# The last stage of a two-layer decoder trunk: its first loads and splits moved ahead, its outputs issued by GpSimd, its norm products cut in pairs

## The chip, the cores and the metric

The kernel runs on one core of a Trainium2 chip. The metric is the time of one execution on the device in microseconds (us), lower is better. The engines are TensorE (PE, with its weight loads shown apart as PEld), VectorE (DVE), ScalarE (ACT), GpSimd (POOL) and SyncE (SP). SP only issues transfers here; ACT and POOL can issue them too, and such an issue stands in that engine's queue like any other instruction. Every queue is worked off in order.

## The reference

Two layers, each `x + mixer(RMSNorm(x))`, over 2048 tokens of width 1024; a last RMSNorm ends the trunk. Layer 0 is an mLSTM, layer 1 an RG-LRU. What the change touches is the second half of layer 1 and the last norm:

```python
xr, g = split(rmsnorm(x, ln_g[1]) @ w_in)            # two halves of width 1536
xc = causal_dwconv(xr)
r  = sigmoid(blockdiag(xc, w_a) + b_a); ig = sigmoid(blockdiag(xc, w_x) + b_x)
log_a = -8 * r * softplus(-lam); a = exp(log_a)
hs = linear_scan(a, sqrt(1 - exp(2*log_a)) * (ig * xc))
x  = x + (hs * silu(g)) @ w_out
out = x * rsqrt(mean(x*x) + eps) * final_g
```

## The kernel before

All matrix products are done in float32 as three products of rounded parts: an operand is split into `hi` (a cast on ACT, L720) and `lo` (a subtraction on DVE, L723), and `mm3` (L347 to L349) adds `hi*hi + hi*lo + lo*hi`. One weight tile of 128x128 against 512 tokens is thus three matmuls.

The stages follow one another: `phase_a1`, `phase_a2` (layer 0), `phase_b1` (output projection of layer 0 and input projection of layer 1), `phase_b2` (gates, scan, output projection and last norm). The change is in the end of `phase_b1` and in `phase_b2`.

**The end of phase_b1.** The input projection runs in groups of seven products (`Slab.group`). The last group makes the last four tiles of the branch `g`: `out(mi, ni, put)` of `g_out` lets `put` write the tile (a copy on ACT for tile (0,0), additions on DVE at L259 for the other three), then applies SiLU on ACT (L1155), and writes the tile to DRAM; for this last group POOL issues that write (L1157).

**phase_b2** goes over four blocks of 512 tokens. In a block there are eight gate steps `("g", b, i)`: step i needs one weight tile of the block-diagonal gates, 128x896 (`wg`, 21 matmuls); even steps make the r gate and the decay (L1286 to L1295), odd ones the input gate, the scan and the split result `yh`, `yl` (L1290 to L1304, then L720 and L723). There are 24 output columns `("r", b, i)`: column i needs one tile of `w_out`, 128x512 (`wr`, 12 matmuls), and the 24 columns make the two halves of the block's output. Columns lag the gates by five steps, and three columns follow each gate step.

*Weights.* `fetch` loads a raw tile on SP (L1232) and splits it. In block 0 POOL writes the split tile to DRAM (L1235), and the later blocks load it from there on SP (L1229). There is one raw buffer for `wg` and three for `wr`, two split buffers for `wg` and four for `wr`. `weights()` keeps three tiles fetched ahead, all with raised priority. `load(b, p)` brings three tiles of `xc` (768 KB): one transfer on SP (L1265), but for the first in the kernel, which is three transfers on POOL (L1262).

*The norm.* After a half's last column, `x2_out` loads four tiles of x on SP (L1345; eight buffers for two halves), adds the products and squares them. Three steps later come the sums and `rsqrt` on POOL (L343), three steps later the row of factors (`stats_rows`, copied on ACT at L1370), the eight products on DVE (L1372) and the eight writes of the result (L1373): on ACT, in the last block in turn on ACT and SP. This tail runs while the next block's columns call `next(run["r", b - 1])`, one piece at each column.

*The order.* The program is traced, and a planner puts each engine's instructions in an order by its own estimate of times and by priority (the program's order, raised by `high_priority`). Buffers are placed in SBUF pool after pool in the order in which the pools are opened, and the pools of phase_b2 lie over those of phase_b1; `reuse_waits="tile"` makes an access wait for the old tile under it alone. So the pool that is opened first lies over the first operands of phase_b1 (`u11`, `t2`, ...), which the last group reads first. `order(first, then)` (already used where phase_a2 begins) adds an edge that puts the instructions of `then` behind those of `first` on the same engine.

Of the kernel before, what the change touches and what calls it, by code (L numbers as in the profile page):

```python
# [7 lines left out]
F32 = mybir.dt.float32  # L8
F32R = mybir.dt.float32r
I32 = mybir.dt.int32  # L10
AF = mybir.ActivationFunctionType
# [3 lines left out]
P = 128  # L15
# [23 lines left out]
class Slab:  # L39
# [20 lines left out]
    def wk(self, name):  # L60
        return self.rg.tile([P, 516], F32, tag="wk", name=name, bufs=10)
# [233 lines left out]
class Trunk:  # L295
# [731 lines left out]
    def phase_b1(self, xT, wout, rwin, D):  # L1027

        tc, nc = self.tc, self.nc
        NG = 6  # L1030
        with ExitStack() as ctx:
            S = Slab(self, ctx, "g1")
            tp, rg, wk, psum = S.tp, S.rg, S.wk, S.psum
# [3 lines left out]
            order = [("w", k, 0) for _ in range(NTB) for k in range(16)]  # L1037
# [5 lines left out]
            ready = []  # L1043
# [104 lines left out]
            def g_out(m2, s):  # L1148
                def out(mi, ni, put):
                    m, n = m2 * 2 + mi, s * 2 + ni  # L1150
                    g = wk("g")[:, 0:TB]
                    put(g)

                    def rest():
                        nc.scalar.activation(g, g, AF.Silu)  # L1155
                        q = nc.gpsimd if s == 1 and m2 == NG - 1 else nc.scalar
                        q.dma_start(D["g"][m, :, n * TB:(n + 1) * TB], g)  # L1157
                    return rest
                return out
# [43 lines left out]
    def phase_b2(self, rgate, rwout, D, outT):  # L1203


        tc, nc = self.tc, self.nc
        NT = 12
        with ExitStack() as ctx:
            wp = ctx.enter_context(tc.tile_pool(name="w4", bufs=4, reuse_waits="tile"))
            tp = ctx.enter_context(tc.tile_pool(name="t4", bufs=2, reuse_waits="tile"))  # L1210
            pm = ctx.enter_context(tc.tile_pool(name="psB", bufs=8, space=PSUM, reuse_waits="tile"))
            steps = []
            lag = 5
# [5 lines left out]
            order = list(steps)  # L1219
            ready = []  # L1220

            def fetch(kind, b, i):

                m = 896 if kind == "g" else 512
                both = wp.tile([P, 2 * m], F32R, tag="w" + kind, name="w" + kind, bufs=2 if kind == "g" else 4)
                wh, wl = both[:, 0:m], both[:, m:2 * m]
                keep = D["gw" if kind == "g" else "ow"][i]
                if b > 0:
                    nc.sync.dma_start(both.bitcast(F32), keep)  # L1229
                    return wh, wl  # L1230
                raw = wp.tile([P, m], F32, tag="wr" + kind, name="wr", bufs=1 if kind == "g" else 3)
                nc.sync.dma_start(raw, rgate[i // 2, :, i % 2 * 896:(i % 2 + 1) * 896] if kind == "g" else  # L1232
                                  rwout[i % NT, :, i // NT * 512:(i // NT + 1) * 512])
                self.split_into(wh, wl, raw, "a", "v")
                nc.gpsimd.dma_start(keep, both.bitcast(F32))  # L1235
                return wh, wl

            def weights():

                with tc.high_priority():  # L1240
                    while order and len(ready) < 3:
                        ready.append(fetch(*order.pop(0)))
                return ready.pop(0)

            def psum(name):
                return pm.tile([P, TB], F32, tag="mm", name=name)
# [7 lines left out]
            def load(b, p):  # L1254

                c = tp.tile([P, 3, TB], F32, tag="xc", name="xc", bufs=4)
                hi = tp.tile([P, 3, TB], F32R, tag="xch", name="xch")
                lo = tp.tile([P, 3, TB], F32R, tag="xcl", name="xcl")
                src = D["xr"][p * 3:p * 3 + 3, :, b * TB:(b + 1) * TB]
                if b == 0 and p == 0:  # L1260
                    for t in range(3):
                        nc.gpsimd.dma_start(c[:, t], src[t])  # L1262
                        self.split_into(hi[:, t], lo[:, t], c[:, t], "a", "v")
                else:
                    nc.sync.dma_start(c, src.rearrange("k p t -> p k t"))  # L1265
                    self.split_into(hi, lo, c, "a", "v")
                return c, hi, lo

# [42 lines left out]
            def block(b):  # L1311

                ys = blocks[b] = []
                if b == 0:
                    with tc.high_priority():
                        xs = load(b, 0)
                else:
                    xs = load(b, 0)
                for p in range(4):
                    nxt = load(b, p + 1) if p < 3 else None  # L1320
                    yield from gates(b, p, xs, ys)
                    xs = nxt

            def x2_out(b):

                bs = slice(b * TB, (b + 1) * TB)
                ys = blocks[b]
                x2, sacc = [], None
                for half in range(2):
                    acc = [psum("acc") for _ in range(4)]  # L1330
                    last = b == NTB - 1 and half == 1
                    held = []
                    for k in range(NT):
                        held.append((k, weights()))
                        if not last or k < NT - 3 or k == NT - 1:
                            for m in range(4):
                                ms = slice(m * P, (m + 1) * P)
                                for i, (wh, wl) in held:
                                    self.mm3(acc[m], wh[:, ms], wl[:, ms], ys[i][0], ys[i][1], i == 0, i == NT - 1)
                            held = []  # L1340
                        if k < NT - 1:
                            yield
                    for m in range(4):
                        x = tp.tile([P, TB], F32, tag="x2", name="x2", bufs=8)
                        nc.sync.dma_start(x, D["x1"][half * 4 + m, :, bs])  # L1345
                        nc.vector.tensor_tensor(x, x, acc[m], op=ALU.add)
                        x2.append(x)
                        if sacc is None:
                            sacc = tp.tile([P, TB], F32, tag="sacc", name="sacc", bufs=1)
                            nc.scalar.activation(sacc, x, AF.Square)  # L1350
                        else:
                            sq = tp.tile([P, TB], F32, tag="sq", name="sq")
                            nc.scalar.activation(sq, x, AF.Square)
                            if last and m == 3:
                                sums = [sacc, sq]
                            else:
                                nc.vector.tensor_tensor(sacc, sacc, sq, op=ALU.add)
                                sums = [sacc]
                    yield
                rc = tp.tile([P, 4], F32, tag="rc", name="rc")  # L1360
                yield
                yield
                self.stats_sum(tp, pm, sums, rc, "mm")
                yield
                yield
                yield
                rb = self.stats_rows(pm, rc, "mm")
                if not last:
                    pb, rb = rb, tp.tile([P, TB], F32, tag="rb", name="rb", bufs=1)
                    nc.scalar.copy(rb, pb)  # L1370
                for m in range(KD):
                    nc.vector.scalar_tensor_tensor(x2[m], x2[m], self.v("gf", m), rb, op0=ALU.mult, op1=ALU.mult)  # L1372
                    (nc.scalar if m % 2 or not last else nc.sync).dma_start(outT[m, :, bs], x2[m])  # L1373

            run = {}
            for kind, b, i in steps:
                if kind == "g":
                    if i == 0:
                        run["g", b] = block(b)
                    next(run["g", b])  # L1380
                else:
                    if i == 0:
                        run["r", b] = x2_out(b)
                    next(run["r", b])
                    if b > 0:
                        next(run["r", b - 1], None)
# [94 lines left out]
```

## Time and profile before

| | |
|---|---|
| median of 3 runs | 3046.7 us (3042.29 to 3050.06) |
| the profiled execution, its own time | 3045.92 us |
| its span in the trace | 3044.1 us |
| PE busy | 2921.0 us (96%) |
| DVE busy | 2083.8 us (68%) |
| ACT busy | 1470.6 us (48%) |
| POOL busy | 195.4 us (6%) |

Times below are us from the start of the span. The page cuts the span in 40 slices; the last stage begins in slice 34, where PE falls to 7 tenths. The views of the trace that follow are the timeline (start, duration, engine, line, what it writes and reads, and in brackets how long the engine stood idle before it and what it waited for), the busy time of each engine in given stretches with the granted clock of PE, groups of instructions by line, and transfers by line.

### The profile page before, as it was taken

How to read it: one execution, taken by the hardware profiler on the slowest of the kernel's cores; microseconds unless marked ns; L12 is line 12 of the kernel's file. 1: busy time of each engine (PE TensorE's matmuls, PEld its weight loads, DVE VectorE, ACT ScalarE, POOL GpSimd, SP SyncE). 2: the span in 40 equal slices, each digit the busy share in tenths (PEclk: the TensorE clock that was granted, in tenths of full speed). 3: DMA queues.
4: the chain of work that ended last, by engine and by line, in shares of the span. 5: the costliest groups of instructions: out<-in, count | busy, mean ns of one | idle time of the engine just before them, and what ended most of it. 6: DMA issues, size and time to landing. Idle time of an engine off the chain costs nothing. (4 is left out here: it accounts for less than half of the span.)

```text
span 3044.1 us, 43340 instructions
## 1 busy us (share of the span) xinstructions
PE 2921.0 (96%) x15730; PEld 2503.5 (82%) x15730; DVE 2083.8 (68%) x3555; ACT 1470.6 (48%) x2458; POOL 195.4 (6%) x409
## 2 busy tenths in 40 slices
PE   7999999999999999999999899999999997899997
PEld 5799987899988898989899777877888886688886
DVE  7766788534566687888888555687778374876663
ACT  6344545323344566666666323243445233865651
POOL 0111110000000011111110000001110000000000
PEclk9999999999999999999999999999999998999998
DMA  6766677667677544454443665566666656888865
GB/s 227 269 214 245 223 245 242 207 203 208 214 236 222 187 139 156 139 163 146 136 146 108 195 190 179 181 209 226 215 215 223 208 185 246 302 282 302 301 206 166
DMA packets 308662, 632.06 MB, mean 208 GB/s; under 512 B 27680, under 2 KB 106272, under 8 KB 308448
## 3 DMA queue, kind: packets, MB, share of 16 engines
q1 hardware_dynamic: 219328, 408.66, 43.2%
q10 hardware_dynamic: 58752, 106.98, 10.0%
q0 software_dynamic: 30368, 113.65, 9.5%
q8 instruction: 124, 2.03, 0.3%
q14 instruction: 90, 0.74, 0.1%
HBM read 407.74 MB, written 221.45 MB: 207 GB/s over the span
## 5 line engine op out<-in xcount | busy, mean ns | idle before, releaser
L720 ACT CAST s<-raw 128x512 fp32r<-128x512 f32 (+1 forms) x360 | 222.7, 621 | 497.5 <-PE acc L349 192.5
L723 DVE TENSOR_TENSOR s<-raw,s 128x512 fp32r<-128x512 f32 (+1 forms) x360 | 247.1, 689 | 94.7 <-ACT s L720 92.3
L347 PE MATMUL acc<-yh,s 128*128 128x512 f32 x512 | 203.0, 399 | 9.9 <-DVE x L1115 3.3
L348 PE MATMUL acc<-yl,s 128*128 128x512 f32 x512 | 203.5, 397 | 0.0
L349 PE MATMUL acc<-yh,s 128*128 128x512 f32 x512 | 203.1, 397 | 0.0
L347 PE MATMUL acc<-yh,wr 128*128 128x512 f32 x384 | 149.3, 397 | 15.1 <-DMA wr<-d_ow 7.7
L348 PE MATMUL acc<-yl,wr 128*128 128x512 f32 x384 | 151.2, 394 | 0.0
L349 PE MATMUL acc<-yh,wr 128*128 128x512 f32 x384 | 150.8, 393 | 0.0
L647 DVE SCALAR_TENSOR_TENSOR xc<-xm,vec,xc 128x512 f32<-128x512 f32 x192 | 140.3, 747 | 14.5 <-ACT xc L645 12.5
L720 ACT CAST s<-sum 128x512 fp32r<-128x512 f32 (+1 forms) x120 | 74.3, 620 | 153.0 <-PE pa L349 48.0
L347 PEld LDWEIGHTS acc<-yh,s 128*128 128x128 f32 x512 | 96.9, 190 | 35.0 <-DVE x L1115 4.4
L348 PEld LDWEIGHTS acc<-yl,s 128*128 128x128 f32 x512 | 97.2, 190 | 23.2 <-DVE yl L723 1.0
L349 PEld LDWEIGHTS acc<-yh,s 128*128 128x128 f32 x512 | 97.0, 189 | 22.7
L915 DVE SCALAR_TENSOR_TENSOR C<-C,dl,kv 128x516 f32<-128x516 f32 x112 | 83.7, 747 | 44.7 <-PE kv L349 44.6
L347 PE MATMUL gate<-xch,wg 128*128 128x512 f32 x224 | 92.7, 417 | 21.5 <-ACT wg L720 11.7
L647 DVE SCALAR_TENSOR_TENSOR xc<-xr,vec,xc 128x512 f32<-128x512 f32 x144 | 105.1, 747 | 7.3 <-ACT xc L645 6.3
L723 DVE TENSOR_TENSOR s<-sum,s 128x512 fp32r<-128x512 f32 (+1 forms) x120 | 82.6, 689 | 39.7 <-ACT s L720 38.2
L720 ACT CAST Ch<-C 128x516 fp32r<-128x516 f32 x120 | 74.8, 623 | 64.7 <-DVE da L933 48.1
L347 PE MATMUL pj<-vwh,xmh 128*128 128x512 f32 x256 | 103.1, 403 | 0.0
L347 PEld LDWEIGHTS acc<-yh,wr 128*128 128x128 f32 x384 | 72.7, 190 | 34.1 <-issue 8.1
L349 PE MATMUL pj<-vwh,xml 128*128 128x512 f32 x256 | 100.3, 392 | 0.0
L348 PE MATMUL pj<-vwl,xmh 128*128 128x512 f32 x256 | 100.0, 391 | 0.0
(429 smaller groups left out, 9435.9 us busy)
## 6 DMA issues: line engine op xcount, KB each, us to landing
wr<-d_ow SPq DMA_DIRECT2D x72, 512.0 KB, 4.3
d_wx<-s POOLq DMA_DIRECT2D x64, 512.0 KB, 4.1
s<-d_wx SPq DMA_DIRECT2D x64, 512.0 KB, 4.1
raw<-in_wout_dram SPq DMA_DIRECT2D x128, 256.0 KB, 3.0
raw<-in_wxz_dram SPq DMA_DIRECT2D x124, 256.0 KB, 4.4
d_wr<-s POOLq DMA_DIRECT2D x48, 512.0 KB, 3.5
s<-d_wr SPq DMA_DIRECT2D x48, 512.0 KB, 4.5
raw<-in_rwin_dram SPq DMA_DIRECT2D x84, 256.0 KB, 3.9
```

Source lines behind the costliest of these rows:

```text
L347: mm(out, sh, mh, start=first, stop=False, skip_group_check=resumed)
L348: mm(out, sh, ml, start=False, stop=False, skip_group_check=resumed)
L349: mm(out, sl, mh, start=False, stop=last, skip_group_check=resumed)
L647: nc.vector.scalar_tensor_tensor(out, x[:, j:j + TB], self.v(wn, m * 4 + j), out, op0=ALU.mult, op1=ALU.add)
L720: a = nc.scalar.copy(hi, src)
L723: b = (nc.gpsimd if lo_eng == "p" else nc.vector).tensor_tensor(lo, src, hi.bitcast(F32), op=ALU.subtract)
L915: nc.vector.scalar_tensor_tensor(C2, C2, self.dl[:, r:r + 1], p2, op0=ALU.mult, op1=ALU.add)
```

## The change

Five edits:

1. In the last group of phase_b1, `g_out` notes the additions and SiLUs of the three tiles after (0,0) in `self.tail`; in `fetch` of the first gate weight, `order(a, self.tail[-4:])` puts its cast on ACT ahead of the last three SiLUs and its subtraction on DVE ahead of the last addition.
2. The gate weights get a pool of their own (`g4`), opened first; then the pool of the activations (`t4`), then that of `w_out` (`w4`). Sizes and numbers of buffers stay.
3. The first `xc` load is one transfer on SP like the others; its three splits stay apart.
4. The columns' weights of block 0 are fetched without raised priority.
5. The writes of the result are issued by POOL in blocks 0 to 2 (in the last block by ACT and SP as before), and `x2_out` yields after every second product, so the eight products are spread over four columns.

```diff
@@ g_out (phase_b1)
                     g = wk("g")[:, 0:TB]
-                    put(g)
+                    end = s == 1 and m2 == NG - 1
+                    if end and (mi, ni) == (0, 0):
+                        self.tail = []
+                    a = put(g)
+                    if end and (mi, ni) != (0, 0):
+                        self.tail.append(a)
 
                     def rest():
-                        nc.scalar.activation(g, g, AF.Silu)
+                        a = nc.scalar.activation(g, g, AF.Silu)
+                        if end and (mi, ni) != (0, 0):
+                            self.tail.append(a)
@@ phase_b2
+            gp = ctx.enter_context(tc.tile_pool(name="g4", bufs=2, reuse_waits="tile"))
+            tp = ctx.enter_context(tc.tile_pool(name="t4", bufs=2, reuse_waits="tile"))
             wp = ctx.enter_context(tc.tile_pool(name="w4", bufs=4, reuse_waits="tile"))
-            tp = ctx.enter_context(tc.tile_pool(name="t4", bufs=2, reuse_waits="tile"))
@@ fetch
-                both = wp.tile([P, 2 * m], F32R, tag="w" + kind, name="w" + kind, bufs=2 if kind == "g" else 4)
+                pool = gp if kind == "g" else wp
+                both = pool.tile([P, 2 * m], F32R, tag="w" + kind, name="w" + kind)
...
-                raw = wp.tile([P, m], F32, tag="wr" + kind, name="wr", bufs=1 if kind == "g" else 3)
+                raw = pool.tile([P, m], F32, tag="wr" + kind, name="wr", bufs=1 if kind == "g" else 3)
...
-                self.split_into(wh, wl, raw, "a", "v")
+                a = self.split_into(wh, wl, raw, "a", "v")
+                if kind == "g" and i == 0:
+                    self.order(a, self.tail[-4:])
@@ weights
-                with tc.high_priority():
-                    while order and len(ready) < 3:
+                while order and len(ready) < 3:
+                    if order[0][0:2] == ("r", 0):
                         ready.append(fetch(*order.pop(0)))
+                    else:
+                        with tc.high_priority():
+                            ready.append(fetch(*order.pop(0)))
@@ load
+                nc.sync.dma_start(c, src.rearrange("k p t -> p k t"))
                 if b == 0 and p == 0:
                     for t in range(3):
-                        nc.gpsimd.dma_start(c[:, t], src[t])
                         self.split_into(hi[:, t], lo[:, t], c[:, t], "a", "v")
                 else:
-                    nc.sync.dma_start(c, src.rearrange("k p t -> p k t"))
                     self.split_into(hi, lo, c, "a", "v")
@@ x2_out
-                    (nc.scalar if m % 2 or not last else nc.sync).dma_start(outT[m, :, bs], x2[m])
+                    (nc.gpsimd if not last else nc.scalar if m % 2 else nc.sync).dma_start(outT[m, :, bs], x2[m])
+                    if m % 2:
+                        yield
```

## Rows read from the trace of the kernel before

**Rows 1.** Busy time of each engine in five stretches of the last stage (block 0 with the start; the rest of blocks 0 and 1; block 2; block 3 to its last gate; the last columns). Columns: length, busy us and number of instructions of each engine, mean granted clock of PE as a share of full speed, busy share of the 16 DMA engines, GB/s.

```profile
2553.00:2675.00 122.00, 96.23 (x365) 73.69 (x366) 82.45 (x70) 94.45 (x119) 14.41 (x27) 0.89 0.88 317
2675.00:2780.00 105.00, 103.88 (x462) 85.02 (x461) 74.34 (x67) 69.78 (x88) 5.82 (x10) 1.00 0.87 302
2780.00:2885.00 105.00, 104.62 (x465) 85.55 (x464) 68.54 (x60) 65.00 (x81) 1.01 (x1) 1.00 0.81 286
2885.00:2976.00 91.00, 91.00 (x406) 74.67 (x404) 57.63 (x52) 49.56 (x62) 1.01 (x1) 1.00 0.67 222
2976.00:3028.00 52.00, 44.01 (x182) 35.65 (x182) 17.20 (x20) 6.09 (x9) 0.00 (x0) 0.90 0.47 156
```

**Rows 2.** Timeline of PE where the last stage begins: the first matmul after each pause. The first row is the first matmul of the stage.

```profile
2559.02 0.79 PE L347 MATMUL gate<-xch,wg 128*128 128x512 f32 x1 [7.69 <-ACT xch L720]
...
2572.06 0.79 PE L347 MATMUL gate<-xch,wg 128*128 128x512 f32 x1 [6.36 <-ACT wg L720]
...
2581.53 0.51 PE L347 MATMUL gate<-xch,wg 128*128 128x512 f32 x1 [0.23 <-ACT wg L720]
...
2589.70 0.79 PE L347 MATMUL gate<-xch,wg 128*128 128x512 f32 x1 [3.08 <-ACT wg L720]
...
2604.76 0.50 PE L347 MATMUL gate<-xch,wg 128*128 128x512 f32 x1 [1.36 <-ACT wg L720]
```

**Rows 3.** The same view as rows 1, for three stretches of 5 us: one at the low clock, one at the full clock, and one in which DVE was busy throughout.

```profile
2560.00:2565.00 5.00, 5.00 (x12) 3.93 (x13) 0.30 (x1) 0.00 (x0) 0.00 (x0) 0.50 1.02 408
...
2605.00:2610.00 5.00, 5.00 (x23) 4.09 (x23) 4.50 (x4) 4.97 (x5) 0.53 (x1) 1.00 0.93 289
...
2620.00:2625.00 5.00, 2.45 (x10) 1.38 (x8) 5.00 (x6) 4.75 (x8) 1.59 (x3) 1.00 0.89 320
```

**Rows 4.** Timeline of POOL at the same place: the last write of `g`, the first two of the three `xc` transfers, and the third.

```profile
2553.02 0.54 POOL L1157 DMA_DIRECT2D d_g<-g  x1 [2.27 <-ACT g L1155]
2553.61 1.08 POOL L1262 DMA_DIRECT2D xc<-d_xr  x2
...
2570.01 0.55 POOL L1262 DMA_DIRECT2D xc<-d_xr  x1
```

**Rows 5.** Timeline of SP's queue at the same place (the duration of a row of several issues runs from the first to the end of the last).

```profile
2535.36 0.33 SPq L1232 DMA_DIRECT2D wr<-in_rgate_dram  x1
2538.16 2.39 SPq L1232 DMA_DIRECT2D wr<-in_rwout_dram  x3
2556.00 0.38 SPq L1294 DMA_DIRECT2D g<-d_g  x1
2556.47 4.50 SPq L1232 DMA_DIRECT2D wr<-in_rwout_dram  x3
2561.02 1.38 SPq L1232 DMA_DIRECT2D wr<-in_rgate_dram  x1
```

**Rows 6.** Timeline of ACT: the second SiLU of the last group, and the casts of the gate weights 0, 1, 2 and 5.

```profile
2546.49 0.63 ACT L1155 ACTIVATE g<-g 128x512 f32<-128x512 f32 x1 [2.23 <-DVE g L259]
...
2552.63 0.92 ACT L720 CAST wg<-wr 128x896 fp32r<-128x896 f32 x1
...
2571.08 0.92 ACT L720 CAST wg<-wr 128x896 fp32r<-128x896 f32 x1
...
2580.55 0.93 ACT L720 CAST wg<-wr 128x896 fp32r<-128x896 f32 x1
...
2603.77 0.93 ACT L720 CAST wg<-wr 128x896 fp32r<-128x896 f32 x1
```

**Rows 7.** Timeline of DVE at the same place: the last two additions of phase_b1 and the subtraction of gate weight 0.

```profile
2548.56 0.69 DVE L259 TENSOR_TENSOR g<-pc,u 128x512 f32<-128x512 f32 x1 [2.11 <-PE pc L349]
2551.37 0.69 DVE L259 TENSOR_TENSOR g<-pd,u 128x512 f32<-128x512 f32 x1 [2.12 <-PE pd L349]
2553.58 1.09 DVE L723 TENSOR_TENSOR wg<-wr,wg 128x896 fp32r<-128x896 f32 x1 [1.52 <-ACT wg L720]
```

**Rows 8.** Transfers issued from 2530 to 2700 us by what they move: number, size, median us from issue to landing.

```profile
wr<-in_rwout_dram SPq DMA_DIRECT2D x24, 256.0 KB, 4.8
...
wr<-in_rgate_dram SPq DMA_DIRECT2D x8, 448.0 KB, 4.8
```

**Rows 9.** Groups of instructions of the last stage by line: busy us and mean ns of one, then idle time before them. The two halves of the split of a column's weight.

```profile
L723 DVE TENSOR_TENSOR wr<-wr 128x512 fp32r<-128x512 f32 x24 | 16.1, 684 | 11.8 <-ACT wr L720 11.6
L720 ACT CAST wr<-wr 128x512 fp32r<-128x512 f32 x24 | 14.4, 617 | 16.7 <-DMA wr<-in_rwout_dram 8.6 <-PE acc L349 7.9
```

**Rows 10.** Timeline of the last change of blocks: ACT, then DVE, then PE.

```profile
2964.38 5.63 ACTq L1373 DMA_DIRECT2D out_dram<-x  x8
2970.04 1.28 ACT L1290 ACT_TABLE_LOAD   x1 [6.48 <-DMA out_dram<-x]
2971.34 1.84 ACT L1290 ACTIVATE ig<-gate,lc 128x512 f32<-128x512 f32 x3
...
2963.60 5.39 DVE L1372 SCALAR_TENSOR_TENSOR x<-x,vec,rb 128x512 f32<-128x512 f32 x8 [0.92 <-ACT rb L1370]
2973.21 1.76 DVE L1297 SCALAR_TENSOR_TENSOR xc<-ig,xc 128x1536 f32<-128x1536 f32 x1 [4.22 <-ACT ig L1290]
...
2967.36 0.40 PE L349 MATMUL gate<-xch,wg 128*128 128x512 f32 x1
...
2983.70 0.76 PE L347 MATMUL acc<-yh,wr 128*128 128x512 f32 x1 [7.70 <-DMA wr<-d_ow]
```

## The prediction

> **What bounds the kernel now.** I began with the busy time by stretches [rows 1]. From 2675 to 2976 us PE hardly pauses: 105.00 - 103.88 = 1.1 us, then 0.4 us, then none. There only PE's work counts. The loss is at both ends. From 2553 to 2675 us 365 matmuls ran; at 23 in 5 us, the full rate [rows 3], they would take 79 to 84 us, so about 38 of 122 us are lost. From 2976 to 3028 us it is 52.00 - 44.01 = 8.0 us of idle time, plus some us at the low clock (granted 0.90). So the change can win only at the start of the last stage and at its last change of blocks.
>
> PE's timeline names the start's waits [rows 2]. The previous stage's last matmul ends at 2559.02 - 7.69 = 2551.33 us. Then PE waits 7.7 us for the cast of `xc`, 6.4 for gate weight 1, and 3.1 and 1.4 for later gate weights. After the long pauses the granted clock is 0.50 (1.2 GHz) and 5 us hold 12 matmuls, not 23 [rows 3].
>
> Two chains stand behind this. **xc:** the last SiLU ends only with the last group, POOL issues its write at 2553.02 and only then the first `xc` transfers; the third stands behind the weights' writes until 2570.01 [rows 4]. **Gate weights:** there is one raw buffer, so weight n+1 is loaded only once weight n is split. Weight 0 is issued at 2535.36 [rows 5], and with the median 4.8 us to landing [rows 8] it is there at about 2540.2; yet its cast runs at 2552.63 [rows 6], behind the SiLUs, and its subtraction ends at 2554.67 [rows 7]. Then SP stands behind the load of `g` (2556.00) and three column weights, so weight 1 is issued at 2561.02 [rows 5] and cast at 2571.08 [rows 6]. From there casts 2 and 5 follow at 2580.55 and 2603.77: 32.7 us for four turns, 8.2 each, where PE needs 21 matmuls, 4.8 us, per weight. Until columns come in, PE follows this chain, so what weight 1 gains is passed on to weight 5.
>
> **The change part by part.**
>
> *Order edge and gate pool (edits 1 and 2).* They add no instruction. The gate pool stays over `u11` and the first of `t2`, so weight 0 is loaded at about 2535.4 as before. Its cast moves ahead of the SiLU at 2546.49 [rows 6]; landed at 2540.2, it fits there in 0.92 us. What now stands behind the cast on ACT is three SiLUs, and behind them only writes of `g`; a cast some us late would cost PE nothing. The subtraction goes behind the addition at 2548.56 (ends 2549.25) and ahead of that at 2551.37 [rows 7]: with 1.09 us it ends at 2550.34, in a gap. Weight 1 can be issued at 2550.4. By the tiles' sizes the first load of `g` now falls on `t4` and `u22` instead of the last group's outputs, so it should no longer hold SP till 2556.00. With 4.8 us to landing weight 1 is cast at 2555.2; with the 10.06 us that it took from issue to cast before (2561.02 to 2571.08), at 2560.5. The shift of the chain is 10.6 to 15.9 us. I take 13, the middle: SP also gives out several 768 KB `xc` loads beside it, but before them DMA is not yet full.
>
> *First xc on SP (edit 3).* Three POOL issues go, one on SP comes, behind weight 1 at 2550.8. 448 + 768 KB at 408 GB/s [rows 3] are 3.0 us; with the 4.8 us of a landing as the upper end, `xc` is there from 2554 to 2556 and PE starts some 1.5 us later, at 2555.5 to 2557.5, not 2559.02. With a cold clock for as long as before (21 matmuls in about 7.6 us) and weight 1 behind them, PE wants weight 2 at about 2569, and the chain brings it at 2581.53 - 13 = 2568.5. So the earlier start is used up by the weights' chain, and nothing is added for it; the missing third tile costs nothing any more either.
>
> *Columns at plain priority (edit 4) and w4 last.* Nothing is added or removed; SP, ACT and DVE may order column weights behind other work. Below: 0 (the first columns are wanted only after gate step 5, near 2592). Above: see the rivals. I take 0, since per column the raw turn is 0.33 + 4.8 + 0.62 + 0.68 = 6.4 us [rows 5, 8, 9] and three buffers make that 2.1 us, against 12 matmuls in 2.7 us.
>
> *DMA.* The first 122 us moved 317 GB/s x 122 us = 38.7 MB [rows 1]; at 408 GB/s [rows 3] that takes 95 us. So no more than 27 us can go; 13 fit.
>
> *Outputs on POOL, products in pairs (edit 5).* ACT loses eight issues per change of blocks, and with them its wait: at the last change it is held from 2964.38 and starts the table load at 2970.04 and the three input gates at 2971.34, though the gates' last matmul ended at 2967.76 [rows 10]. Without that the third input gate is done one activation (1.84 / 3 us) later, at 2968.4. DVE's products end at 2968.99 if all eight still run first; so L1297 starts at 2969.0 instead of 2973.21, and PE's 7.7 us stall is shortened by 4.2 us. It stays 3.5 us: what follows (scan, `g`, `yh`) is the same work. If the pairs let L1297 go first, it is 4.7; if the clock then stays up, up to 4.4 more (44.01 us busy for 182 matmuls, 39.6 at the full rate) [rows 1, 3]. A gain of nothing would need POOL to hold DVE, and it does not wait for DVE's later work. The two earlier changes have 1.1 + 0.4 us of idle time [rows 1]; I take 1. POOL has 24 issues more at 0.53 us, and was busy 5.8 of 105 us there; behind them in its queue stands only the next block's `rsqrt`, a block later.
>
> Here a rule speaks against the edit. Three POOL issues took 1.59 us in a stretch in which DVE was busy 5.00 of 5 us [rows 3]: 0.53 each, no delay. The Trainium skill, "SBUF — State Buffer", section "SBUF: two separate sides", says that a transfer issued by GpSimd waits for its descriptors while DVE runs an operation in a two-port mode. By the row this edit's sum stays; by the rule each of eight issues could be held by one DVE operation, as a rival below works out.
>
> **Sum:** 13 + 4.2 + 1 = 18.2 us off the profiled execution's 3045.92 us is 3027.7 us. That execution lies 0.8 us below the median, so I say 3028 us.
>
> **The rivals.**
>
> A. *The start is filled again by DMA.* From 2560 us DMA was full (share 1.02, 408 GB/s) [rows 3]. If all `xc`, `g` and x loads go out at 2551 us ahead of weight 2 (3.1 + 1.6 MB, 11.5 us at that rate), weight 2 comes as late as 2573 to 2577 us and the start gains 5 to 8 us. Against it: weight loads keep their raised priority. With the last change: 3045.9 - 6 - 3 = 3037 to 3042 us. Chance 0.17.
>
> B. *The start does not move at all* because the first loads of the activations are still put behind the writes of `g` (that was so in POOL's queue, and the whole stage begins where the last group ends). Only edit 5 counts: 3041 us. Chance 0.08.
>
> C. *Columns starve PE: slower.* In block 0 SP's queue stands behind a blocked gate weight or x load while column weights wait at plain priority. With one raw buffer in flight a column takes 6.4 us, with two 3.2, with three 2.1. PE's columns and gates together have 2.7 + 1.6 = 4.3 us per column. From fewer than 1.5 buffers in flight on, PE waits; at one, 2.1 us x 24 columns = 50 us are lost, at 1.2 (5.3 us) 24 us. That gives 3028 + 24 to 50, about 3052 to 3078 us; I put it at 3060. For it: PE already lost about 10 us between 2605 and 2675 us [rows 1, 2]. Against it: loads go out when a buffer is free, whatever the priority. Chance 0.10.
>
> D. *POOL's issues are held by DVE.* By rows: eight issues each held by one L1297 (1.76 us) are 18 us where the products took 5.4. The x loads and the column weights behind them on SP come 13 us late, four split buffers cover 4 x 2.7 = 11, so 2 us at each of three changes: 3034 us. Chance 0.03; it is the page's rule.
>
> **How the numbers follow.** My forecast, 3018 to 3037 us, has 0.62; A 0.17, B 0.08, C 0.10, D 0.03. About 0.3% (9.1 us) is what a measurement of this kernel can tell from no change: faster means under 3037.6 us. Forecast, D and a fifth of A give faster 0.68; the rest of A, B and a little of C same 0.22; C slower 0.10. The range: the low end takes the upper bounds together, 15.9 + 4.7 + 4.4 + 1.5 = 26.5 us, which is 3019 us, and some us more if PE no longer falls to the low clock at the start: 3016 us; the high end covers A and B, 3043 us. Outside lie C and a rest, under 0.2.
>
> **What would show it.** Right: the cast of gate weight 0 before 2547 us on ACT, weight 1 issued near 2550.5 and cast from 2555 to 2561 us; the first gate matmul before 2558 us; the first matmul of gate weight 5 near 2592 us instead of 2604.76; no wait of ACT for the result's writes, and a last stall of PE of 3 to 4 us. Wrong: gate casts more than 9 us apart (A), `xc` issued after 2553 us (B), PE waiting for L720 of `wr` in block 0 (C), POOL issues above 1 us or SP waiting longer for the result's writes before L1345 (D).

## The result, and the profile after

The changed kernel takes 3057.9 us (median of 7 runs, 3054.04 to 3060.64) against 3046.6 us for the kernel before (7 runs, 3042.29 to 3050.06): ratio 1.0038, 95% interval 1.0027 to 1.0049. It is 11.4 us slower by the medians, where 18 us less were forecast. Its profiled execution took 3060.64 us, with a span of 3058.9 us.

PE's timeline of the last stage after the change: the first matmul behind four of its pauses. These rows answer to [rows 2], and the last one to PE's row in [rows 10].

```profile
2567.57 0.80 PE L347 MATMUL gate<-xch,wg 128*128 128x512 f32 x1 [14.91 <-ACT xch L720]
...
2615.61 0.79 PE L347 MATMUL acc<-yh,wr 128*128 128x512 f32 x1 [5.82 <-ACT wr L720]
...
2675.07 2.07 PE L347 MATMUL acc<-yh,wr 128*128 128x512 f32 x4 [2.50 <-ACT yh L720]
...
2999.41 2.08 PE L347 MATMUL acc<-yh,wr 128*128 128x512 f32 x4 [3.34 <-ACT yh L720]
```

Between the first and the third row stand also 7.15 us for `wg` (2597.08), 1.72 for `R` (2621.11) and 6.33 for `wr` (2648.24). The stage's first pause has doubled (14.91 against 7.69 us), and waits for `wr`, of which before had none, cost 12.2 us. The last stall is 3.34 us instead of 7.70.

Where the time went is read at matched points. The first write of the result (end of block 0's tail) was issued at these times, before on ACT, after on POOL (timelines of the two engines, before first):

```profile
2749.55 6.34 ACTq L1373 DMA_DIRECT2D out_dram<-x  x8
```
```profile
2769.07 4.32 POOL L1386 DMA_DIRECT2D out_dram<-x  x8 [13.50 <-DVE x L1385]
```

The previous stage's last matmul ended at 2551.33 us before and at 2567.57 - 14.91 = 2552.66 after. So from there to the first write it took 198.2 us before and 216.4 after: 18.2 us lost in block 0. From that write to the start of the last stall it is 2976.00 - 2749.55 = 226.5 before, 2996.07 - 2769.07 = 227.0 after. The last stall gives 4.4 us back, and the rest of the span (60.4 against 59.5 us) 0.9. The whole stage has become 506.2 us long instead of 492.8.

Block 0 splits at gate weight 5. Before, its cast began 2603.77 - 2551.33 = 52.4 us into the stage, after 2602.55 - 2552.66 = 49.9: up to there the change was still 2.5 us ahead. It was lost behind this point, where the columns come in. PE from the end of weight 5's cast to the first write, before and after (columns as in [rows 1]):

```profile
2604.76:2749.55 144.79, 137.74 (x593) 110.83 (x594) 111.36 (x97) 111.30 (x140) 13.26 (x24) 0.99 0.84 296
```
```profile
2603.50:2769.10 165.60, 149.22 (x613) 119.41 (x612) 117.18 (x104) 116.27 (x147) 15.41 (x29) 0.92 0.80 280
```

Of the 20.8 us, 165.60 - 149.22 - (144.79 - 137.74) = 9.3 are more idle time and 11.5 more busy time. The window after holds 20 gate matmuls more, some 4.3 us at the full rate of 23 in 5 us [rows 3]; the other 7 us are the same work at a granted clock of 0.92 instead of 0.99. The 5 us from 2616 on, behind the pause for `wr`, held 8 matmuls (3.38 us busy) at clock 0.50 (1.2 GHz). Over the whole window DMA was less busy than before (0.80 against 0.84).

SP's queue at the start of the stage, answering to [rows 5]:

```profile
2536.69 21.47 SPq L1241 DMA_DIRECT2D wr<-in_rgate_dram  x3
2558.26 0.92 SPq L1274 DMA_DIRECT2D xc<-d_xr  x2
...
2577.57 1.68 SPq L1241 DMA_DIRECT2D wr<-in_rwout_dram  x3
2579.30 6.53 SPq L1358 DMA_DIRECT2D x<-d_x  x7
2587.28 0.33 SPq L1241 DMA_DIRECT2D wr<-in_rgate_dram  x1
```

Three gate weights stand ahead of the first `xc`. The third can go out only once weight 1 is subtracted (DVE, 2556.71 + 1.09 us), so `xc` is issued at 2558.26. ACT, answering to [rows 6]:

```profile
2545.49 0.93 ACT L720 CAST wg<-wr 128x896 fp32r<-128x896 f32 x1
...
2555.74 0.94 ACT L720 CAST wg<-wr 128x896 fp32r<-128x896 f32 x1 [1.69 <-DMA wr<-in_rgate_dram]
2566.90 1.66 ACT L720 CAST xch<-xc 128x512 fp32r<-128x512 f32 x3 [10.22 <-DMA xc<-d_xr]
...
2575.08 0.94 ACT L720 CAST wg<-wr 128x896 fp32r<-128x896 f32 x1
...
2596.09 0.94 ACT L720 CAST wg<-wr 128x896 fp32r<-128x896 f32 x1 [5.95 <-DMA wr<-in_rgate_dram]
...
2612.72 0.94 ACT L720 CAST wg<-wr 128x896 fp32r<-128x896 f32 x1 [2.91 <-DMA wr<-in_rgate_dram]
...
2614.94 0.61 ACT L720 CAST wr<-wr 128x512 fp32r<-128x512 f32 x1
```

The last row is the first cast of a column weight. Its raw tile was issued at 2577.57, with three of them the buffers were full, and the cast stood in ACT's queue behind gate casts for which ACT sat idle (5.95, 2.91 us). Before, these casts came early, ahead of PE's first column matmul (2606.24 us):

```profile
2553.46 1.65 ACT L720 CAST wr<-wr 128x512 fp32r<-128x512 f32 x3
2567.84 0.62 ACT L720 CAST wr<-wr 128x512 fp32r<-128x512 f32 x1 [8.29 <-DMA wr<-in_rwout_dram]
```

The second pause for `wr` (6.33 us, at 2648.24) has another cause: there the cast, of the sixth column weight, waited for its transfer. After the change, on SP and on ACT:

```profile
2633.52 6.57 SPq L1241 DMA_DIRECT2D wr<-in_rwout_dram  x3
```
```profile
2647.57 0.62 ACT L720 CAST wr<-wr 128x512 fp32r<-128x512 f32 x1 [5.30 <-DMA wr<-in_rwout_dram]
```

The first of these three loads went out when DVE had subtracted the third column weight (2632.65 + 0.68 us) and so freed its raw buffer. It landed 14.0 us after its issue, with DMA busy at a share of 0.91 from 2634 to 2648 us; the median landing before was 4.8 us [rows 8].

### The profile page after: what moved, and what is told of

It is laid out like the page before. It is cut to its first block, busy times and chain, and to the rows that moved or that the text cites. A ratio compares the mean times of both kernels' runs of the same rounds, so it can differ in the third digit from the quotient of the medians.

```text
span 3058.9 us, 43349 instructions
## 1 busy us (share of the span) xinstructions
PE 2928.0 (96%) x15730; PEld 2507.2 (82%) x15730; DVE 2084.5 (68%) x3555; ACT 1470.7 (48%) x2458; POOL 206.9 (7%) x430
## 5 line engine op out<-in xcount | busy, mean ns | idle before, releaser
L347 PE MATMUL acc<-yh,wr 128*128 128x512 f32 x384 | 154.8, 408 | 18.6 <-ACT wr L720 12.2
```

The costliest lines, as they stand in the source:

```text
L347: mm(out, sh, mh, start=first, stop=False, skip_group_check=resumed)
```

## Experiments

Theory 1: edit 4 is the loss, since columns at plain priority are split too late. Theory 2: the place of the first `xc` behind the gate weights (edits 2 and 3) is the loss. Edit 5 would gain its 4 us under both. All twelve kernels beside each other; "to write" and "stage" are the distances from the previous stage's last matmul to the first write of the result and to the end of the span, worked out from one profiled execution of each kernel as above (before: 198.2 and 492.8; after: 216.4 and 506.2). Each ratio is to the kernel before, run again beside that kernel (medians 3044.67 to 3045.28 us).

| kernel | median us | ratio to before (interval) | to write | stage |
|---|---|---|---|---|
| after without edit 4 | 3048.24 | 1.0008 (0.9999 to 1.0017) | 203.6 | 493.3 |
| before with edit 4 | 3056.38 | 1.0038 (1.0025 to 1.005) | 209.6 | 500.6 |
| before with edits 1 to 3 | 3051.81 | 1.0024 (1.0014 to 1.0034) | 202.5 | 499.1 |
| before with edit 5 | 3041.03 | 0.9992 (0.9983 to 1.0001) | 199.5 | 491.9 |
| before, writes on POOL only | 3042.21 | 0.9991 (0.9981 to 1.0) | 199.2 | 488.8 |
| before, pairs only | 3045.42 | 1.0 (0.9992 to 1.0009) | 198.0 | 491.4 |
| after, own pool for `xc` | 3049.12 | 1.0013 (1.0004 to 1.0021) | 206.3 | 498.6 |
| the same without edit 4 | 3041.21 | 0.9987 (0.9978 to 0.9996) | 200.5 | 491.8 |
| and `w4` ahead of `t4` | 3050.34 | 1.0019 (1.001 to 1.0027) | 207.0 | 494.3 |
| instead a second raw gate buffer | 3039.75 | 0.9982 (0.9973 to 0.9991) | 195.2 | 486.2 |
| instead x loads held back | 3037.29 | 0.9969 (0.9957 to 0.9981) | 191.3 | 480.5 |
| both of these | 3039.45 | 0.9985 (0.9977 to 0.9994) | 196.4 | 489.1 |

**Edit 4, undone in after.**

```diff
-                while order and len(ready) < 3:
-                    if order[0][0:2] == ("r", 0):
-                        ready.append(fetch(*order.pop(0)))
-                    else:
-                        with tc.high_priority():
-                            ready.append(fetch(*order.pop(0)))
+                with tc.high_priority():
+                    while order and len(ready) < 3:
+                        ready.append(fetch(*order.pop(0)))
```

> The changed kernel with edit 4 undone (columns' weights of block 0 at raised priority again). Theory 1: PE no longer waits for ACT's cast of a column weight (12.2 us in all in the changed kernel), and the time is 8 to 16 us under the changed kernel, 3042 to 3050 us. Rival 2 (the transfers are the bound: DMA is full from 2556 us on, and any order gives the same): within 4 us of the changed kernel, with other pauses in place of those. Rival 3 (priority puts three column weights ahead of gate weight 2, as before): the gate chain slips by 5 us or more and the time is half way, 3050 to 3055 us.

1.0008. Columns were cast from 2567.26 us on, and no wait for `wr` is left in the group of PE's matmuls (busy, mean ns, idle and what ended it, from 2553 to 2690 us; after first, then this kernel):

```profile
L347 PE MATMUL acc<-yh,wr 128*128 128x512 f32 x51 | 23.3, 469 | 14.7 <-ACT wr L720 12.2 <-ACT yh L720 2.5
```
```profile
L347 PE MATMUL acc<-yh,wr 128*128 128x512 f32 x62 | 24.7, 418 | 7.1 <-ACT yh L720 3.9 <-ACT R L1296 3.2
```

The first pause stays (14.64 us for `xch`). So edit 4 costs 0.3% here, and what is left of the change is no gain.

**Edit 4 alone, in before** (the same lines the other way).

> The kernel before with edit 4 alone. Theory 1 (plain priority makes the columns' casts late on ACT and their loads late on SP): PE waits for column weights in block 0 for 6 to 14 us, partly paid by earlier gate weights (no longer behind three column weights on SP); the time is 3 to 12 us over before. Rival 4 (plain priority is harmless in itself and only hurts beside the moved pool of column weights): within 3 us of before or faster.

1.0038, as much as the whole change. Three columns were cast at 2552.84, and the next only at 2626.89, behind the last gate weight's cast (2617.55). Their loads came late too: three raw buffers were free from 2555.87 us on, but the next three loads went out at 2577.19, before at 2556.47 [rows 5]. The first write came 11.4 us later in the stage than before. PE's waits for casts of `wr` between 2553 and 2690 us are only 4.6 us of that, less than the 6 to 14 expected; 1.7 us for subtractions of `wr`, 2.7 for `xcl` (2657.83) and 2.8 for `x` (2734.39) stand beside them. That edit 4 costs by itself is shown. Whether the late load or the late split weighs more was not run apart.

**Edits 1 to 3 alone** (after with edits 4 and 5 undone).

> The kernel before with edits 1 to 3 alone (order edge, pools, first xc on SP). Theory 1 (the order on SP, xc behind three gate weights, takes back what the earlier gate weights gain; edits 4 and 5 add up with it): the changed kernel with edit 4 undone lies at a ratio of 1.0008 and edit 5 alone at 0.9992, so this one lies near 1.0016, 3047 to 3053 us, with a first pause of PE of 14 to 15 us. Rival 5 (edit 5 costs once the start has changed): 3043 to 3046 us.

1.0024: a loss too. SP gives out three gate weights (2538.33, 21.60 us) ahead of `xc` (2560.02), PE's first pause is 14.57 us and gate weight 3 is missed by 6.52. Theory 2 holds as well. The parts sum to 0.38 + 0.24 - 0.08 = 0.54%, and the whole change costs 0.38. The intervals are wide enough for this to be noise; that the two losses overlap, since both starve PE in the same block, is likely but not shown.

**Edit 5 alone, and its halves.**

```diff
-                    (nc.scalar if m % 2 or not last else nc.sync).dma_start(outT[m, :, bs], x2[m])
+                    (nc.gpsimd if not last else nc.scalar if m % 2 else nc.sync).dma_start(outT[m, :, bs], x2[m])
+                    if m % 2:
+                        yield
```

> The kernel before with edit 5 alone (result written by GpSimd's queue, norm products in pairs). Theory 1 (the loss is in block 0: columns' weights at plain priority, and xc behind three gate weights on SP): the gain at the changes of blocks is there, PE's last stall falls from 7.7 us to 3 to 4 us, and the time is 4 to 7 us under before. Rival (edit 5 costs, its writes or later products disturb the next block): the time is 2 us or more over before, with new pauses of PE after 2750 us.

> Before, with the result's writes of blocks 0 to 2 issued by GpSimd, but no yield between the products (one half of edit 5). If the writes on ACT's queue are what the 4 us of the last change come from: last stall of PE near 3.5 to 4.5 instead of 7.7, 3040 to 3043 us. If the pairs do it (the scan's multiplication may go ahead of products): stall stays near 7 and the time at 3044 to 3046. If POOL is held by DVE: single POOL issues of the result above 1 us.

> Before, with the products yielded in pairs, but the writes still issued by ACT (the other half of edit 5). If only the issues on ACT matter: the last stall stays at 6 to 8 us or grows, 3044 to 3048 us. If the pairs matter: stall 3 to 5 us, 3040 to 3043.

Edit 5 gives 0.9992, the writes on POOL alone 0.9991, the pairs alone 1.0: the gain of some 3 us is at the edge of what was measured. By the medians the writes carry it, though the intervals overlap. In the first two PE's last stall is 3.48 us. With pairs alone it is 3.48 too, but 2.16 us for `wr<-d_ow` follow. At the last change the eight products run in one go in every kernel (after: DVE 5.39 us from 2983.54), so the yields spread no product there. With pairs alone they did let ACT's table load go ahead of six of the eight writes:

```profile
2966.02 1.04 ACTq L1373 DMA_DIRECT2D out_dram<-x  x2
2967.10 1.28 ACT L1290 ACT_TABLE_LOAD   x1 [1.89 <-DVE x L1372]
```

POOL's issues in after, all 24 of them (min, median and max in ns):

```profile
L1386 POOL DMA_DIRECT2D out_dram<-x x24: 539/539/594, 2769.1 to 2989.2; - x24
```

At the last change they were issued from 2984.59 on, while DVE ran the products and then L1310 without a gap; none was held, so rival D has nothing for it in this trace. The Trainium skill, "SBUF — State Buffer", section "SBUF: two separate sides", has the hold for DVE operations in a two-port mode; no run here shows in which mode these ran.

**A pool of its own for xc, right behind the gate weights'**, in after.

```diff
             gp = ctx.enter_context(tc.tile_pool(name="g4", bufs=2, reuse_waits="tile"))
+            xp = ctx.enter_context(tc.tile_pool(name="x4", bufs=2, reuse_waits="tile"))
...
-                hi = tp.tile([P, 3, TB], F32R, tag="xch", name="xch")
+                hi = xp.tile([P, 3, TB], F32R, tag="xch", name="xch")
```

(`xc` and `xcl` likewise.)

> The changed kernel with the xc tiles and their split parts in a pool of their own, opened right behind the gate weights' pool, so that the first xc load need not be put behind the end of the previous stage. Theory 1: on SP the first xc load comes second, ahead of gate weight 1, and lands before the previous stage ends; PE's first pause falls from 14.9 us to under 4 us. As the gate weights then set the pace, the time falls by 5 to 11 us against the changed kernel, to 3047 to 3053 us, and the two waits for column weights stay. Rival 2 (transfers bound): the pause moves to the next gate weights, under 3 us of gain.

1.0013, 0.25% off the loss. SP now issues `xc` ahead of weight 1, and PE goes from the previous stage into this one almost without a stop:

```profile
2536.35 0.33 SPq L1242 DMA_DIRECT2D wr<-in_rgate_dram  x1
2537.05 3.86 SPq L1275 DMA_DIRECT2D xc<-d_xr  x2
2551.26 0.34 SPq L1242 DMA_DIRECT2D wr<-in_rgate_dram  x1
```
```profile
2553.70 0.49 PE L348 MATMUL gate<-xcl,wg 128*128 128x512 f32 x1 [1.15 <-DVE xcl L723]
2568.70 0.80 PE L347 MATMUL gate<-xch,wg 128*128 128x512 f32 x1 [5.39 <-ACT wg L720]
```

So the order of the pools sets the place of `xc`; that it does so by what the tile's memory lies over is inferred. PE still waits 8.08 us for `wr`: edit 4.

**The same without edit 4.**

> The changed kernel with both repairs: xc in a pool of its own behind the gate weights' pool, and the columns' weights of block 0 at raised priority. Theory 1 (two causes that add up): 9.7 and 8.8 us come off, 3037 to 3043 us, under the kernel before; the first pause of PE is under 4 us. Rival 2 (the transfers bound block 0 in the end, or the repairs win the same time): 3045 to 3049 us, the pauses moved to gate weights 2 to 4.

0.9987: of the kernels built on the change, the first that is faster than the kernel before. What is left are waits for gate weights, 7.52 us for weight 2 and 9.04 for weight 4. Weight 2 landed 11.4 us after its issue (2556.88), with DMA full (share 1.04 from 2560 to 2575 us) and before the first x load (2574.00).

**Then w4 opened ahead of t4.**

> As the kernel with both repairs, with the columns' pool opened ahead of the activations' pool, so that the first three column weights are loaded while the previous stage still multiplies. Theory 1 (the gate weights' single raw buffer sets the pace from weight 1 on): the same time within 3 us, since column weights are not what PE waits for once they have priority. Rival 2 (transfers bound the start): 3 to 6 us faster, since 768 KB leave the full stretch.

1.0019, a miss: the same time within 3 us, or 3 to 6 us less, was expected. Gate casts now stand on ACT ahead of gate activations and wait there for their transfers; PE waits 4.83 us for `R` and 5.43, 3.42 and 3.00 for `ig`.

**Instead a second raw buffer for gate weights** (`bufs=2 if kind == "g"`; two small tiles cut to one buffer to make room).

> As the kernel with both repairs, with a second raw buffer for gate weights (two small tiles of the norm go from two buffers to one to make room). Theory 1 (the chain load, cast, subtract, load of one raw buffer sets the pace of gate weights 1 to 5, 8.2 us each where PE needs 4.8): 5 to 10 us faster than with both repairs, 3030 to 3036 us, and gate casts 5 to 7 us apart. Rival 2 (transfers bound it): within 3 us, casts still 8 us apart with landings twice as late.

0.9982, another miss: 1.5 us under the kernel with one buffer, where theory 1 had 5 to 10. The gate casts from 2556.58 to 2596.62 us are still 8.0 us apart, as rival 2 had it. PE no longer waits for weight 2 and only 1.77 us for weight 3, but a pause of 9.93 us for `ig` (2579.70) takes their place. ACT had sat idle 4.63 us ahead of that work, for the transfer of a column weight whose cast stood first (2572.69).

**Instead block 0's x loads held behind the last raw gate weight.**

```diff
-                nc.sync.dma_start(raw, rgate[i // 2, :, i % 2 * 896:(i % 2 + 1) * 896] if kind == "g" else
+                ld = nc.sync.dma_start(raw, rgate[i // 2, :, i % 2 * 896:(i % 2 + 1) * 896] if kind == "g" else
...
+                if kind == "g":
+                    self.ld = ld
...
-                        nc.sync.dma_start(x, D["x1"][half * 4 + m, :, bs])
+                        ld = nc.sync.dma_start(x, D["x1"][half * 4 + m, :, bs])
+                        if b == 0:
+                            self.order([self.ld], [ld])
```

> The kernel of the run with xc's own pool and raised priority for the columns, with one more edge: block 0's eight loads of x go out on SP only behind the raw load of the last gate weight. In that run five x loads (2574.00, 5.92 us) stood ahead of gate weight 4's raw load (2580.01), whose cast came only at 2591.91, and PE waited 9.04 us for it. Theory 1, x loads hold the weight: weight 4 is issued near 2574 and cast near 2584, PE's 9.04 us fall to 2 to 5, and the time is 3036 to 3038 us (ratio to before 0.9965 to 0.998). Theory 2, a turn of the single raw buffer takes 8 to 10 us whatever stands ahead: weight 4 is cast after 2588 and the time stays at 3039 to 3043. Theory 3, the moved x loads now hold the first column weights behind them: waits of PE for casts of wr near 2620 and the time is above 3043.

> The same edge on the run with a second raw buffer for the gate weights (3039.75 us; gate casts some 8 us apart from 2540.69 to 2596.62). Theory 1: six x loads (2576.93, 7.15 us) stood ahead of a gate raw load at 2585.29, but with two raw buffers that load is two weights ahead of use, so little moves: 3038 to 3041 us. Theory 2, the traffic of the x loads is what stretches the casts to 8 us: the casts after 2575 are 6 us apart and the time is 3034 to 3037.

The first has the lowest median: 3037.29 us, ratio 0.9969, a stage of 480.5 us. It has five runs only, and its interval overlaps that of the kernel without the edge. Weight 4 costs PE 3.33 us instead of 9.04. But it was not issued sooner: both kernels send it 2.1 to 2.2 us after the cast of weight 3. It landed sooner. SP and ACT without the edge, then with it:

```profile
2574.00 5.92 SPq L1356 DMA_DIRECT2D x<-d_x  x5
2580.01 0.43 SPq L1242 DMA_DIRECT2D wr<-in_rgate_dram  x1
...
2591.91 0.94 ACT L720 CAST wg<-wr 128x896 fp32r<-128x896 f32 x1 [7.21 <-DMA wr<-in_rgate_dram]
```
```profile
2584.41 8.71 SPq L1242 DMA_DIRECT2D wr<-in_rgate_dram  x2
...
2590.70 0.94 ACT L720 CAST wg<-wr 128x896 fp32r<-128x896 f32 x1 [2.21 <-DMA wr<-in_rgate_dram]
```

From issue to cast 11.9 us became 6.3. From 2574 to 2592 us DMA was full without the edge (share 1.00, 381 GB/s), and less so with it (0.91); the eight x loads are 2.1 MB, 5.5 us at the first rate. The wait for weight 2 stayed (7.82 us). With two raw buffers the edge brought nothing (0.9985 against 0.9982), as expected there. Both kernels with two buffers have a pause for `ig` (9.93 and 7.40 us) and one of 6.2 us for `xcl` near 2644 us, which the edge alone has not; why they do was not tried further.

## Why the prediction was wrong

It was wrong in sign: rival C came true, which had 0.10 with 3060 us.

**Edit 4, "I take 0", failed.** The raw turn was summed as issue, landing, cast and subtraction, 6.4 us, of which three buffers make 2.1. Left out was the time that a landed tile lies until its cast comes up in ACT's queue: from issue to cast it was 2614.94 - 2577.57 = 37.4 us. The landing was mis-sized too: the sixth column weight took 14.0 us, not 4.8. The raised priority had moved the split as well as the load, and with it four columns lay split before PE came to the first; without it the columns start with nothing in stock and wait for `wr`. Rival C had the result and part of the cause. Column loads did stand behind a blocked gate weight on SP (2577.18), and "loads go out when a buffer is free, whatever the priority", put against C, did not hold. But the loads were in time for the first column; it waited for ACT's queue, which C does not name. Alone edit 4 costs 0.38%, in this change 0.30%.

**"xc ... behind weight 1 at 2550.8" failed.** It came behind weight 2 at 2558.26. The step rested on no row of when its memory comes free or where it stands in SP's order; that it was the order of the pools is shown by the kernel with a pool of its own, though which tile held it up is inferred. Its landing was mis-sized too: with 4.8 us as the upper end, `xc` was cast 8.6 us after issue, DMA being full from 2553 to 2575 us (share 0.99). PE began at 2567.57, not 2555.5 to 2557.5.

**The start's -13 failed with it.** Its first links held: weight 0 was cast at 2545.49 and weight 1 at 2555.74, both as forecast. But "the chain brings" weight 2 at 2568.5 took the weights' chain to run by itself. Its raw tile landed 4.9 us after its issue, but its cast stood on ACT behind the cast of `xc` and the first gate's activations, and came at 2575.08, not at 2580.55 - 13 = 2567.6. By weight 5, 2.5 us of 13 were left. Even with `xc` in time and edit 4 undone the gain was 0.13%. There the transfers that rival A named held the weights: weight 2 landed 11.4 us after its issue, before any x load, and weight 4 11.8 us after, behind five of them. Of these transfers a run moved only the x loads away.

**Edit 5 held.** The last stall fell by 4.4 us (4.2 forecast), ACT no longer waited for writes, POOL was not held. The 1 us at the two earlier changes did not come: the first has pauses of 0.56 and 0.83 us (2783.35 and 2785.14) where 1.12 stood before, the second one of 0.83 us (2893.97) where 0.38 stood.

## What to carry to other kernels

A priority covers everything traced under it: before lowering one, ask not when the tile is wanted but what its load and its split will stand behind in each in-order queue, and how large the stock is when the first consumer comes. An early load is early only if its memory is free: read the pool order for the tile that the first matmul needs, ahead of those that follow. And a chain of loads, casts and products through shared queues is not shifted as a block; the first link that is late sets all later ones.

## What was not expected of the hardware

The previous stage's last matmul ended anywhere from 2547.6 us (second raw buffer and x loads held back) to 2555.0 (x loads held back) in these executions, though the change lies almost wholly behind it: 7 us of scatter ahead of the stage, larger than most effects here. The seven runs of the kernel before lie as far apart (3042.29 to 3050.06 us). Distances within the stage tell more than single times.

SP needed 5.92 us for five issues of x loads while DMA was full, 1.2 us each, where an issue by itself took 0.33 to 0.4. A full DMA alone does not explain it: the gate weight issued right behind them took 0.43 us.
